# One store for tiles 16 to 31 in a matmul with scale and add, and one load of x moved ahead of addends

## The chip, the cores and the metric

The kernel runs on one core of one Trainium2 chip. The metric is the device time of one execution in microseconds (us), the median of several runs. The profile is one execution taken by the hardware profiler; its times count from the start of its span.

## What is computed

```python
batch, m, k, n = 16, 512, 1024, 768
return (scale * np.matmul(x, weight) + add_value).astype(np.float32)
```

All inputs and the output are float32, scale is 0.1. Flattened, x is 8192 rows of 1024, weight 1024 x 768, and add_value and the result 8192 rows of 768.

## The kernel before, in words

**Tiles.** The 8192 rows are cut into 64 tiles of 128. Rows are dealt out in groups of 2048: partition p of a group holds 16 consecutive rows, and tile t is row t mod 16 of every partition. Consecutive tiles of a group are therefore consecutive rows in memory, and one transfer of n tiles moves n rows in one stretch for each partition.

**Buffers.** `xs` has 16 slots for tiles of x (tile t in slot t mod 16). `ao` has 32 slots (t mod 32) that hold a tile's addends first and then, in the same place, its result, until that is stored. The addends of tile t + 32 may be loaded only when the result of tile t has been stored.

**What a tile passes through.** SyncE issues nearly all loads and stores. For every 4 tiles (a move), ScalarE and GpSimd each make 8 casts of x to bf16, into `va` (`mover`, L166, two buffers), and count them in `by_act` and `by_pool`. VectorE transposes two tiles at a time from `va` to `xt` (`turn`, L187). TensorE multiplies a tile with 8 weight loads and 16 matmuls into one of four PSUM buffers `mm` (L217, L219). VectorE then finishes two tiles in one instruction, scale * mm + addends, in place in `ao` (`finish`, L196), and counts them in `made`.

**VectorE's order.** For each group of 8 tiles it waits once for the group's addends (L201, `a_sem`), then runs finish, turn, finish, turn, and so on; the turn that follows the finish of tiles t and t + 1 prepares tiles t + 4 and t + 5. A late finish holds up the turn behind it. TensorE waits ahead of every second tile for the turn of its x and for the finish that frees its PSUM buffer (`tensor_engine`).

**SyncE's order.** `STREAM`, written out by hand, lists the transfers: "w" weights, "x" tiles of x, "a" addends, "o" results, "a+" only adjusts a count. An entry ("o", 16, 8) stores tiles 16 to 23. `sync_engine` (L99) goes through the list and issues each entry when its waits are met, so an entry that waits holds all behind it. All of these go into one DMA queue, q1. The waits (`need`, L104) are:

- x: the casts, by both engines, of the tiles whose slots it takes (for 56 to 59: of tile 43 and all before), issue at L120.
- addends: the landing of all addends issued before, and the landing of the store that frees their slots, issue at L133. For 48 to 55 this is the store that holds tile 23, for 56 to 63 the one that holds tile 31.
- results: the landing of the store two entries back, and `made` of their last tile, issue at L146.

The wait for the freeing store is found from the list itself:

```python
t = max(t for t in range(s - A_SLOTS, last + 1 - A_SLOTS) if t not in PAIR)
i = next(j for j, (a, b) in enumerate(stores) if a <= t < a + b)
need(o_sem[i % 2], 16 * (i // 2 + 1))
```

Stores from tile 48 on signal a semaphore of their own, for which the program waits at its end (L261). Tiles 14 and 15 are stored by GpSimd (L96).

Of the kernel before, what the change touches and what calls it, by code (L numbers as in the profile page):

```python
# [22 lines left out]
    ("w", 0, 4), ("w", 4, 4), ("a", 0, 8),  # L23
    ("x", 8, 8), ("a", 8, 8), ("x", 16, 8), ("a", 16, 16), ("x", 24, 8),
    ("x", 32, 8), ("a+", 16, 16), ("o", 0, 14), ("x", 40, 8), ("a", 32, 8),
    ("x", 48, 8), ("a", 40, 8), ("o", 16, 8), ("o", 24, 8), ("a", 48, 8), ("x", 56, 4),
    ("x", 60, 4), ("a", 56, 8), ("o", 32, 16), ("o", 48, 12),
    ("o", 60, 4),
]
# [267 lines left out]
```

## Time and profile before

| | |
|---|---|
| time, median of 3 runs | 206.8 us (206.76 to 206.86) |
| the profiled execution | 206.82 us, of which the span is 205.5 us |
| granted TensorE clock, mean | 0.990 |
| moved from and to HBM | 87.04 MB, 424 GB/s over the span |
| first matmul starts | 26.03 us |
| last finish (tiles 62 and 63) starts | 196.80 us |

In rows of the profile, PE is TensorE, PEld its weight loads, DVE VectorE, ACT ScalarE, POOL GpSimd; SPq is SyncE's queue of instructions, and L146 is line 146. A timeline row has the start, the duration, what ran, how often (x), and in brackets the engine's idle time just before it with what ended that. A row of DMA issues has the count, the size of one, and the median time from issue to landing. DMA and GB/s lines cut a stretch into 40 equal slices; a digit is the busy share in tenths.

### The profile page before, as it was taken

Reading aid. Unit: us, or ns where it says so; the run is one execution under the profiler, and the core shown is the slowest. Engines: PE = TensorE matmul, PEld = TensorE weight load, DVE = VectorE, ACT = ScalarE, POOL = GpSimd, SP = SyncE. Lnnn points to the kernel's source line nnn. Section 1 sums busy time; section 2 is a strip of 40 time slices with the busy share of each in tenths; the row PEclk is TensorE's granted clock in tenths of the full one; section 3 lists DMA queues with packets and bytes.
Section 4 is the critical chain, followed back from the end, with each engine's and each line's share of the span. In section 5 each row is a group of like instructions: output and inputs, shape, how many; then the busy total and the mean of one; then the engine's idle time right before and its main releaser. Section 6 shows DMA issues by size and latency. Waiting matters only on the chain.

```text
span 205.5 us, 2241 instructions
## 1 busy us (share of the span) xinstructions
PE 169.1 (82%) x1024; PEld 50.5 (25%) x512; DVE 97.8 (48%) x66; ACT 134.7 (66%) x129; POOL 137.4 (67%) x135
## 2 busy tenths in 40 slices
PE   0000099999999999999999979999999999999920
PEld 0000023332233322333223322332233332333300
DVE  0004523556555555555555346555555555555330
ACT  2049980699999906999999693959694099930000
POOL 0049994699999916999999995959694099940000
PEclk9999999999999999999999999999999999999996
DMA  7989999999999899999999999999999999998997
GB/s 287 427 375 455 421 485 408 397 439 459 440 459 459 364 453 408 408 402 410 484 390 430 446 416 470 408 435 411 454 426 408 437 459 402 517 431 364 431 459 308
DMA packets 3921, 87.04 MB, mean 424 GB/s; under 512 B 464, under 2 KB 464, under 8 KB 1104
## 3 DMA queue, kind: packets, MB, share of 16 engines
q1 hardware_dynamic: 3712, 86.25, 98.2%
q0 software_dynamic: 208, 0.79, 0.9%
q14 instruction: 1, 0.01, 0.0%
HBM read 61.87 MB, written 25.17 MB: 424 GB/s over the span
## 4 chain that ended last, share of the span: by engine, by line
PE 82%; DMA 6%; ACT 5%; DVE 2%; issue 1%; DVEq 0%; ACTq 0%
PE mm L219 82%; DMA xs<-in_x_dram 6%; ACT va L166 5%; DVE xt L187 1%; DVE ao L196 1%; DVEq L193 0%; DVEq L196 0%; DVEq L185 0%; ACTq L159 0%
## 5 line engine op out<-in xcount | busy, mean ns | idle before, releaser
L219 PE MATMUL mm<-w_bf,xt 128*128 128x512 bf16 (+1 forms) x1024 | 169.1, 329 | 27.6 <-DVE xt L187 27.6
L166 POOL CAST va<-xs 32x1024 bf16<-32x1024 f32 x128 | 135.2, 1056 | 44.3 <-DMA xs<-in_x_dram 31.1
L166 ACT CAST va<-xs 32x1024 bf16<-32x1024 f32 x128 | 133.4, 1042 | 45.3 <-DMA xs<-in_x_dram 33.0
L196 DVE SCALAR_TENSOR_TENSOR ao<-mm,ao 128x1536 f32 (+1 forms) x32 | 56.2, 1756 | 79.3 <-PE mm L219 73.4
L217 PEld LDWEIGHTS <-xt 128*128 128x128 bf16 x512 | 50.5, 99 | 145.7 <-issue 117.5
L187 DVE STREAM_TRANSPOSE xt<-va 128x1024 f32<-128x1024 f32 x32 | 39.4, 1234 | 3.3 <-ACT va L166 2.1
L180 DVE CAST w_bf<-ao 128x3072 bf16<-128x3072 f32 x2 | 4.5, 2245 | 18.1 <-DMA ao<-in_weight_dram 18.1
L155 ACT ACT_TABLE_LOAD x1 | 1.3, 1283 | 1.3 <-SPq L251 1.3
L96 POOL DMA_DIRECT2D out_dram<-ao x3 | 2.0, 671 | 0.0
L278 POOL MEMSET const-float32-0.0<- 128x1 f32 x1 | 0.1, 97 | 0.2 <-issue 0.2
L278 POOL MEMSET const-bfloat16-1.0<- 128x1 bf16 x1 | 0.1, 100 | 0.0
L278 POOL MEMSET const-float32-1.0<- 128x1 f32 x1 | 0.1, 98 | 0.0
L278 POOL MEMSET const-uint8-127<- 128x1 uint8 x1 | 0.1, 98 | 0.0
## 6 DMA issues: line engine op xcount, KB each, us to landing
xs<-in_x_dram SPq DMA_DIRECT2D x7, 4096.0 KB, 16.7
ao<-in_add_value_dram SPq DMA_DIRECT2D x6, 3072.0 KB, 17.0
ao<-in_add_value_dram SPq DMA_DIRECT2D x1, 6144.0 KB, 24.2
out_dram<-ao SPq DMA_DIRECT2D x2, 3072.0 KB, 27.5
out_dram<-ao SPq DMA_DIRECT2D x1, 6144.0 KB, 31.2
out_dram<-ao SPq DMA_DIRECT2D x1, 5376.0 KB, 28.8
out_dram<-ao SPq DMA_DIRECT2D x1, 4608.0 KB, 13.6
xs<-in_x_dram SPq DMA_DIRECT2D x2, 2048.0 KB, 21.1
```

The lines of the kernel that those rows point to most:

```text
L96: move = eng.dma_start(out_v[p:p + n, 0, pair, :], ao[p:p + n, pair, :], max_dma_last_dim=4 * N)
L155: eng.preload_act_table(mybir.ActivationFunctionType.Copy)
L166: copy(va[q % VA_BUFS][32 * b:32 * b + 32, :, a, :], src[32 * a:32 * a + 32, :, b, :]).then_inc(count, 1)
L180: eng.tensor_copy(w_bf[:, s:s + n, :], ao[:, W_AT + s:W_AT + s + n, :]).then_inc(casts, n)
L187: eng.transpose(xt[:, 2 * half:2 * half + 2, :, :].rearrange("p i c m -> p (i c m)"), va[move % VA_BUFS][:, q:q + 2 * KC, :, :].bitcast(fp ...
L196: eng.scalar_tensor_tensor(a, mm[:, q:q + 2, 0:N], float(scale), a, op0=mybir.AluOpType.mult, op1=mybir.AluOpType.add).then_inc(made, 2)
L217: eng.ldweights(x_j, tile_position=(0, 0))
L219: m = eng.add_instruction(mybir.InstMatmult(start_tensor_calc=(j == 0), stop_tensor_calc=(j == KJ - 1), tile_size=(P, P), tile_position=(0 ...
L278: nc = _bacc.Bacc("TRN2", target_bir_lowering=False, num_devices=1)
```

## The change

Two stores of 8 tiles (16 to 23 and 24 to 31) become one of 16, and the load of x of tiles 56 to 59, which stood behind the addends of 48 to 55, now stands ahead of them, right behind the merged store. The order before was: store 16 to 23, store 24 to 31, addends 48 to 55, x 56 to 59, x 60 to 63. It is now: store 16 to 31, x 56 to 59, addends 48 to 55, x 60 to 63. The addends of 48 to 55 now wait for the landing of the merged store. Nothing changes on the other engines; their instructions and order are the same.

```diff
     ("x", 32, 8), ("a+", 16, 16), ("o", 0, 14), ("x", 40, 8), ("a", 32, 8),
-    ("x", 48, 8), ("a", 40, 8), ("o", 16, 8), ("o", 24, 8), ("a", 48, 8), ("x", 56, 4),
+    ("x", 48, 8), ("a", 40, 8), ("o", 16, 16), ("x", 56, 4), ("a", 48, 8),
     ("x", 60, 4), ("a", 56, 8), ("o", 32, 16), ("o", 48, 12),
     ("o", 60, 4),
 ]
```

## Prediction

> **What bounds the kernel now.** I read the page first (engine shares, slices, queues), then the DMA issues one at a time with their time to landing, then VectorE's and TensorE's timelines around the changed stores and at the end.
>
> ```profile
> PE 169.1 (82%) x1024; PEld 50.5 (25%) x512; DVE 97.8 (48%) x66; ACT 134.7 (66%) x129; POOL 137.4 (67%) x135
> DMA  7989999999999899999999999999999999998997
> q1 hardware_dynamic: 3712, 86.25, 98.2%
> PE 82%; DMA 6%; ACT 5%; DVE 2%; issue 1%; DVEq 0%; ACTq 0%
> ```
>
> Two resources stand close to full. The chain that ended last is 82% TensorE, but SyncE's queue q1 moves 86.25 MB and fills 98.2% of what 16 DMA engines have, from the second slice to the last. So a microsecond in which q1 has nothing to move is a microsecond on the end, and TensorE matters where it holds a store back. The issues and landings show how the queue is fed. Each first fence row is an issue (start, duration), and the second fence holds, in the same order, the time from that issue to its landing.
>
> ```profile
> 102.00 0.33 SPq L133 DMA_DIRECT2D ao<-in_add_value_dram  x1
> ...
> 120.42 0.33 SPq L133 DMA_DIRECT2D ao<-in_add_value_dram  x1
> 120.80 0.43 SPq L146 DMA_DIRECT2D out_dram<-ao  x1
> 121.27 0.43 SPq L146 DMA_DIRECT2D out_dram<-ao  x1
> 144.81 0.34 SPq L133 DMA_DIRECT2D ao<-in_add_value_dram  x1
> 145.26 0.57 SPq L120 DMA_DIRECT2D xs<-in_x_dram  x1
> 145.93 0.60 SPq L120 DMA_DIRECT2D xs<-in_x_dram  x1
> 159.36 0.33 SPq L133 DMA_DIRECT2D ao<-in_add_value_dram  x1
> 159.74 0.42 SPq L146 DMA_DIRECT2D out_dram<-ao  x1
> 188.18 0.34 SPq L146 DMA_DIRECT2D out_dram<-ao  x1
> 198.63 0.33 SPq L146 DMA_DIRECT2D out_dram<-ao  x1
> ```
>
> ```profile
> ao<-in_add_value_dram SPq DMA_DIRECT2D x1, 3072.0 KB, 18.4
> ...
> ao<-in_add_value_dram SPq DMA_DIRECT2D x1, 3072.0 KB, 17.0
> out_dram<-ao SPq DMA_DIRECT2D x1, 3072.0 KB, 23.9
> out_dram<-ao SPq DMA_DIRECT2D x1, 3072.0 KB, 31.0
> ao<-in_add_value_dram SPq DMA_DIRECT2D x1, 3072.0 KB, 14.5
> xs<-in_x_dram SPq DMA_DIRECT2D x1, 2048.0 KB, 19.0
> xs<-in_x_dram SPq DMA_DIRECT2D x1, 2048.0 KB, 23.2
> ao<-in_add_value_dram SPq DMA_DIRECT2D x1, 3072.0 KB, 17.1
> out_dram<-ao SPq DMA_DIRECT2D x1, 6144.0 KB, 31.2
> out_dram<-ao SPq DMA_DIRECT2D x1, 4608.0 KB, 13.6
> out_dram<-ao SPq DMA_DIRECT2D x1, 1536.0 KB, 6.8
> ```
>
> Issue plus time gives the landings: addends of 32 to 39 at 120.4, of 40 to 47 at 137.4; stores of 16 to 23 at 144.7, of 24 to 31 at 152.3; addends of 48 to 55 at 159.3; x of 56 to 59 at 164.3, of 60 to 63 at 169.1; addends of 56 to 63 at 176.5; stores of 32 to 47 at 190.9, of 48 to 59 at 201.8, of 60 to 63 at 205.4. They land in the order of issue, spaced by their bytes: 3072 KB take 7.0 to 7.6 us, 2048 KB 4.8 to 5.0, 6144 KB 14.4. So q1 works transfer after transfer and is nowhere empty. The time of a landing is a sum of what stands ahead of it.
>
> **The change part by part.** The profiled execution took 206.82 us with a span of 205.5; the median of the runs shown is 206.8, so the sum is made on 206.82.
>
> *The merge.* Both old stores were issued back to back, at 120.80 and 121.27, so tile 31 was already finished at the first one; the merged store waits for no more than they did. One issue of 0.43 us goes from SyncE, hidden beside a full queue: 0 on the path. The bytes are the same. Whether one transfer of 6144 KB is cheaper in the queue than two of 3072: the two took 152.3 − 137.4 = 14.9 us, the single store of 32 to 47 took 190.9 − 176.5 = 14.4. Bounds are 0 and 0.5; I take 0 for the sum, since those landings carry rounding on every side, and keep 0.5 for the low end. A loss has no row here.
>
> *The wait.* The addends of 48 to 55 go into the slots of tiles 16 to 23, which were free at 144.7. Now they are free when the whole merged store has landed, at 152.3: 7.6 us later. In the old queue the store of 24 to 31 stood ahead of these addends anyway, so that alone moves no byte. It only means that something else must be in the queue while SyncE waits.
>
> *The moved load.* That is x of 56 to 59. It needs xs slots whose tiles (40 to 43) have been cast by both ScalarE and GpSimd.
>
> ```profile
> 109.25 15.27 POOL L166 CAST va<-xs 32x1024 bf16<-32x1024 f32 x14
> ```
>
> GpSimd's run of casts ends at 109.25 + 15.27 = 124.5; the next begins with tiles 44 to 47. So this load is issued at about 124.6 instead of 145.26, and stands in q1 right behind the merged store, 27 us before it is its turn. Behind SyncE's wait for these casts stands only the addends' issue, which waits until 152.3 in any case. The load covers q1 for some 4.9 us from 152.3, the addends' issue at 152.4 needs 1.0 us to start (below): no hole. x of 60 to 63 follows at 153, the addends of 56 to 63 at the landing of those of 48 to 55, as before, under cover of that x load (4.8 us).
>
> Hence the queue's order changes in one place: x of 56 to 59 and the addends of 48 to 55 swap. Old landings 159.3 (addends), 164.3 (x); new ones 157.2 (x), and 164.3 (addends), because the two together take the same 12.0 us. All later landings stay. The x load, 7 us earlier, lets ScalarE and GpSimd cast these tiles sooner, but TensorE never waited for them: after 123.72 it runs without a gap (row below). Gain 0. **The addends' loss, 5.0 us, is the question.**
>
> ```profile
> 111.86 1.76 DVE L196 SCALAR_TENSOR_TENSOR ao<-mm,ao 128x1536 f32 x1 [2.29 <-PE mm L219]
> ...
> 120.75 1.76 DVE L196 SCALAR_TENSOR_TENSOR ao<-mm,ao 128x1536 f32 x1 [5.98 <-DMA ao<-in_add_value_dram]
> 122.42 1.24 DVE L187 STREAM_TRANSPOSE xt<-va 128x1024 f32<-128x1024 f32 x1
> ...
> 160.56 1.76 DVE L196 SCALAR_TENSOR_TENSOR ao<-mm,ao 128x1536 f32 x1 [2.42 <-PE mm L219]
> ```
>
> ```profile
> 123.72 72.97 PE L219 MATMUL mm<-w_bf,xt 128*128 128x512 bf16 x448 [1.60 <-DVE xt L187]
> ```
>
> VectorE finishes tiles 48 and 49 at 160.56 today, 1.3 us after their addends landed, held by TensorE alone. With addends at 164.3 it waits for them. The trace holds the same event: the addends of 32 to 39 landed at 120.4, the finish of 32 and 33 began at 120.75 (0.35 later), the transpose behind it on VectorE (tiles 36 and 37) followed, and TensorE, which had caught up, started tile 36 at 123.72 after 1.60 us of nothing: 123.72 − 120.75 = 2.97 from finish to TensorE. Applied here: finish at 164.3 + 0.35 = 164.65, TensorE ready for tile 52 at 167.6. It would have been there at 123.72 + 16 tiles of 72.97 / 28 = 2.606 us, that is 165.4. **TensorE stalls 2.2 us**, and since it has no gap afterwards, it is late by that to the end. In other words the finish comes 4.1 us late (164.65 against 160.56), and TensorE's look-ahead hides 1.9 of it. In the old event the finish was due two tiles (5.2 us) after the one at 111.86, at 117.1; it was 3.7 late, TensorE lost 1.6, and 2.1 was hidden. The two agree within 0.2.
>
> *What late TensorE does to the queue.* The store of 48 to 59 is issued when tile 59 is finished:
>
> ```profile
> 0.73 0.38 SPq L248 DMA_DIRECT2D xs<-in_x_dram  x1
> ...
> 186.40 1.76 DVE L196 SCALAR_TENSOR_TENSOR ao<-mm,ao 128x1536 f32<-128x1536 f32 x1 [2.26 <-PE mm L219]
> ...
> 196.80 1.76 DVE L196 SCALAR_TENSOR_TENSOR ao<-mm,ao 128x1536 f32<-128x1536 f32 x1 [3.44 <-PE mm L219]
> ```
>
> 186.40 + 1.76 = 188.16, issue at 188.18; likewise 198.56 and 198.63 for the last store. Three looks at the DMA bytes in slices of 0.05 us tell how long an issue takes to move its first piece: the stretches begin at 0.7, 188.8 and 200.2, and slices of bytes count a piece at its start.
>
> ```profile
> GB/s 0 0 0 0 0 0 0 0 0 0 0 0 0 0 0 0 0 0 0 0 655 2621 0 1311 1966 655 655 0 655 0 0 655 655 0 0 0 0 0 655 0
> ...
> GB/s 0 0 0 0 0 0 0 0 0 0 0 0 0 0 0 0 0 0 0 0 737 737 737 0 737 0 1475 1475 1475 0 1475 1475 737 737 0 0 0 0 0 0
> ...
> GB/s 0 0 0 0 0 0 0 0 0 0 246 0 246 0 246 0 492 492 737 492 492 737 0 492 0 492 492 737 492 492 737 0 492 0 492 492 737 246 492 737
> ```
>
> The very first load, into an empty queue, is issued at 0.73 and starts in slice 21, between 1.70 and 1.75: **1.0 us**. The store of 48 to 59 starts in slice 21 from 188.8, between 189.80 and 189.85, when the store ahead lets go of its first engine: 1.65 after its issue, so it has 0.65 to spare. The last store starts in slice 11 from 200.2, at 200.7, 2.1 after its issue: 1.1 to spare. Both issues now come 2.2 us later. The first loses 2.2 − 0.65 = 1.5 us of empty queue; the second, counted alone, would lose 2.2 − 1.1 = 1.1, but it stands behind a store that is itself 1.5 late, so it adds nothing. Sum: 0 (merge) + 0 (x earlier) + 1.5 (empty queue at 190 us) = **206.82 + 1.5 = 208.3 us**.
>
> Bounds of the 1.5: the last store alone forces 1.1, less 0.5 if the merge saves that: 0.6. Upward, the first load took 12.1 us to land by the page's kind of row (4096 KB, from an empty queue), which by the later stores' pace of (201.8 − 190.9) / 4608 KB × 4096 = 9.7 us holds 2.4 us of starting and landing; the store of 48 to 59 would then land at 190.4 + 2.4 + 10.9 = 203.7, 1.9 late.
>
> ```profile
> xs<-in_x_dram SPq DMA_DIRECT2D x1, 4096.0 KB, 12.1
> ```
>
> The Trainium skill, "DMA: Bandwidth & Descriptors", section "Specifications", states about 0.6 us to the first byte for a transfer that SyncE issues; the trace has 1.0 here. By the page's figure the sum would be an estimated 1.1 in place of 1.5, or 207.9 us.
>
> **The rivals.**
>
> *A transfer pays a fixed price, and the merge saves one* (faster). If a saving s comes off the queue ahead of the addends, they land s earlier, the stall shrinks by s, and the end moves by 1.5 − s; this decides for faster from s = 1.9 on (0.4 us is 0.2% of 206.8). With all of the 2.4 us of the first load saved, the stall is gone, the store of 48 to 59 is issued at 188.18 into a queue that is already free and starts at 189.2 instead of 189.8: 206.2 us. Against it: 14.9 against 14.4 us above, and the last two stores, 10.9 us for 4608 KB and 3.6 for 1536, which leave 3.6 − 10.9 / 3 = 0.0 for a fixed part. The Trainium skill, same page, section "Anatomy of one DMA", gives, for transfers that GpSimd issues, a fit with about 2.0 us fixed for each; by that estimate s is 2.0 and the time 206.3. In a queue that is never empty the rows show nothing of it. Chance 0.06: 0.04 faster, 0.02 within 0.2%.
>
> *The lateness is absorbed* (no change, 206.8). The addends come 5.0 us later but VectorE is idle half of the span, and the final stores have some room. For it the look-ahead would have to hide 4.1 − 0.65 = 3.5 us of the late finish; at 120.75 it hid 2.1 of 3.7. Chance 0.07: 0.05 within 0.2%, 0.02 slightly slower.
>
> *The empty queue costs more* (208.7). The store that begins in an empty queue pays the 2.4 us of the first load: + 1.9. For it, one row; against it, that load was the first of the program. Chance 0.12.
>
> That the change doesn't take effect (x of 56 to 59 not early enough to cover the wait) would need its casts after 151; they end at 124.5. I give it nothing.
>
> **How the numbers follow.** The forecast, 208.3, has 0.75, with a range of its own from 207.4 (0.6 late) to 208.7 (1.9 late). A measurement of this kernel tells about 0.2% from no change, 206.4 to 207.2. Faster 0.04, the same 0.02 + 0.05 = 0.07, slower 0.75 + 0.12 + 0.02 = 0.89. The range of 207.3 to 208.9 holds the forecast's bounds and the dearer start, with 0.1 to 0.2 for landings known to a tenth; what it leaves out, some 0.15, is the first rival and the absorption.
>
> **What would show it.** In the profile after: x of 56 to 59 issued at 124.6 and landed at 157; the addends of 48 to 55 issued at 152.4 and landed at 164.3; a second wait of VectorE for addends, ahead of a finish at 164.65; a TensorE gap of 2.2 us that ends at 167.6; the store of 48 to 59 issued at 190.4, with q1 empty for some 1.5 us ahead of it; the last issue at 200.8; a span of 207.0. I am wrong if the addends land before 162, if TensorE shows no second gap, or if the landing of 32 to 47 moves ahead of 190.4.

## The result, and the profile after

The changed kernel takes 207.91 us (median of 14 runs, 207.78 to 209.62) against 206.83 for the kernel before, a ratio of 1.0062 over all runs (the medians alone give 1.0052) with a 95% interval of 1.0044 to 1.0081: 0.6% slower. The profiled execution took 208.01 us with a span of 206.7; its span is 1.2 us longer.

The page of the changed kernel, beside the lines shown ahead: TensorE has as much work as before, more idle time, and q1 a smaller share of the longer span. In the second line each digit is the queue's busy tenth of one fortieth; the new eights are slices 30 and 35 (150 to 155 us and 176 to 181 us). Slice 37, with 190 us in it, was an 8 before too, so this line does not show what happens there; finer slices below do.

```profile
PE 168.6 (82%) x1024; PEld 50.3 (24%) x512; DVE 97.6 (47%) x66; ACT 134.7 (65%) x129; POOL 137.4 (66%) x135
DMA  7999999999999999999999999999989999898997
q1 hardware_dynamic: 3568, 86.25, 97.5%
```

The issues of the moved load, of the addends of 48 to 55, and of the last two stores, from SyncE's timeline, and below them in the same order the DMA rows with the time to landing:

```profile
124.56 0.33 SPq L120 DMA_DIRECT2D xs<-in_x_dram  x1
...
152.26 0.33 SPq L133 DMA_DIRECT2D ao<-in_add_value_dram  x1
...
190.33 0.34 SPq L146 DMA_DIRECT2D out_dram<-ao  x1
...
200.78 0.33 SPq L146 DMA_DIRECT2D out_dram<-ao  x1
```

```profile
xs<-in_x_dram SPq DMA_DIRECT2D x1, 2048.0 KB, 32.3
...
ao<-in_add_value_dram SPq DMA_DIRECT2D x1, 3072.0 KB, 11.9
...
out_dram<-ao SPq DMA_DIRECT2D x1, 4608.0 KB, 12.4
...
out_dram<-ao SPq DMA_DIRECT2D x1, 1536.0 KB, 5.9
```

The x load lands at 156.9 instead of 164.3, the addends at 164.2 instead of 159.3, the two stores at 202.7 and 206.7 instead of 201.8 and 205.4. VectorE's waits and its finish of tiles 48 and 49, then TensorE's timeline, show what the late addends did:

```profile
DVE ao L196 <- DMA ao<-in_add_value_dram: 12.9, 2, 6.5
```

```profile
164.49 1.76 DVE L196 SCALAR_TENSOR_TENSOR ao<-mm,ao 128x1536 f32 x1 [6.48 <-DMA ao<-in_add_value_dram]
166.17 1.23 DVE L187 STREAM_TRANSPOSE xt<-va 128x1024 f32<-128x1024 f32 x1
```

```profile
123.58 41.77 PE L219 MATMUL mm<-w_bf,xt 128*128 128x512 bf16 x256 [2.08 <-DVE xt L187]
167.46 31.38 PE L219 MATMUL mm<-w_bf,xt 128*128 128x512 bf16 x192 [2.10 <-DVE xt L187]
```

VectorE now waits for addends twice (6.0 us once before). The bracket of a TensorE row holds the idle time ahead of it: one gap of 1.60 us before, two now, the second of 2.10 us at tile 52, released by the transpose of its x, which stood behind the finish, which waited for the addends. The last look is the queue at the end. The stretch from 188.8 to 192.8 in slices of 0.1 us, first of the kernel before, then of the changed one; bytes count a piece at its start:

```profile
GB/s 0 0 0 0 0 0 0 0 0 0 737 369 369 1475 737 1475 737 0 0 0 0 0 0 0 737 737 737 1475 737 1106 369 0 0 0 0 0 0 369 737 369
```

```profile
GB/s 0 0 0 0 0 0 0 0 0 0 0 0 0 0 0 0 0 0 0 0 0 0 0 2580 2949 369 0 0 0 0 0 0 0 0 0 0 0 3318 2580 0
```

Before, the 16 engines take up the store of 48 to 59 one after another between 189.8 and 190.5, each as it lets go of the store ahead, which landed at 190.9 to 191.0 in both kernels. Now none starts until 191.1, and then all within 0.3 us. That is the empty queue.

One thing was not forecast. Of the 14 runs eleven lie between 207.78 and 208.2, and three between 209.41 and 209.62. The experiments show where such a second group comes from (below). The kernel before has one too, 0.7 us higher: nine of its 14 runs lie between 206.55 and 206.97, five between 207.21 and 207.50. Between the middles of the lower groups, 206.69 and 207.89, lie 1.2 us, as between the two profiled spans. One run of the kernel before with the early addends (below) took 473.51 us, for which nothing on record gives a cause; its ratio leaves it out.

### The profile page after: what moved, and what is told of

Read it like the earlier page. It is cut to its first block, busy times and chain, and to the rows that moved or that the text cites. A ratio compares the mean times of both kernels' runs of the same rounds, so it can differ in the third digit from the quotient of the medians.

```text
span 206.7 us, 2239 instructions
## 1 busy us (share of the span) xinstructions
PE 168.6 (82%) x1024; PEld 50.3 (24%) x512; DVE 97.6 (47%) x66; ACT 134.7 (65%) x129; POOL 137.4 (66%) x135
```

## The experiments

**Order theory:** the swap makes the addends of 48 to 55 late, VectorE's finish and the transpose behind it hold TensorE, and q1 runs empty ahead of the store of 48 to 59. **Store theory:** the merged store, coarser and landing later, is the cost. **TensorE theory:** the end is late because TensorE is, whatever the queue does.

### The swap without the merge

```diff
-("o", 16, 16), ("x", 56, 4), ("a", 48, 8),
+("o", 16, 8), ("o", 24, 8), ("x", 56, 4), ("a", 48, 8),
```

> The two old stores of 8 tiles, but x of 56 to 59 ahead of the addends of 48 to 55. Order theory (the swap alone makes the addends late, TensorE stalls, q1 runs empty ahead of the store of 48 to 59): addends land near 164.2, a second TensorE gap of 2.1 us, 207.9 us. Store theory (the merge is the cost): 206.8 us.

208.83 us, ratio 1.0085 (1.0052 to 1.0117). The six runs fall in two groups: 207.80, 207.96, 208.09, which is the changed kernel's time, and 209.56, 209.61, 209.66. The profiled execution is of the upper group. Its TensorE timeline and its windows (columns: stretch and its length, then busy time of PE, PEld, DVE, ACT and POOL, the granted clock, DMA share, GB/s):

```profile
167.36 33.05 PE L219 MATMUL mm<-w_bf,xt 128*128 128x512 bf16 x192 [1.99 <-DVE xt L187]
```

```profile
164.00:168.00 4.00, 2.01 (x13) 0.57 (x6) 3.61 (x3) 2.52 (x3) 2.76 (x3) 1.00 1.05 446
168.00:172.00 4.00, 4.00 (x17) 1.02 (x8) 2.09 (x2) 1.79 (x2) 1.69 (x2) 0.57 1.06 455
```

The second stretch in the profile of the changed kernel, for comparison:

```profile
168.00:172.00 4.00, 4.00 (x26) 1.25 (x13) 2.19 (x2) 1.69 (x2) 1.59 (x2) 1.00 1.07 461
```

The gap is there with the old stores, so the swap alone makes it, and the store theory falls. After the gap the granted clock is 0.57 on average over 4 us: the trace has it at 0.5 from 168.20 to 171.61, for 3.41 us, and only 17 matmuls start in the stretch where 26 did. In all, the last 192 matmuls take 33.05 us where the changed kernel's took 31.38, 1.67 more. TensorE is then that much later still, and so is the store: the upper group is the lower one plus 1.6 us. This is the changed kernel's second group too, as far as its times show; no profile of it fell there.

### The merge without the swap

```diff
-("o", 16, 16), ("x", 56, 4), ("a", 48, 8),
+("o", 16, 16), ("a", 48, 8), ("x", 56, 4),
```

> The merged store with the old order behind it: addends of 48 to 55, then x of 56 to 59. Queue theory (the end is late by the time in which q1 is empty, wherever that is): the addends' issue waits until 152.3 with nothing left in q1, so q1 is empty for about 1.6 us near 152, the addends land near 160.7, early enough that TensorE has no second gap; the store of 48 to 59 is issued near 188.2 and finds q1 busy; about 208.1 us. TensorE theory (the end is late because TensorE ends late): no second gap, so 206.8 us. Store theory (the merged store itself costs the 1.1 us): 207.9 us.

210.63 us, ratio 1.0178 (1.0157 to 1.0199). TensorE has no second gap:

```profile
26.37 95.28 PE L219 MATMUL mm<-w_bf,xt 128*128 128x512 bf16 x576 [26.37 <-DVE xt L187]
124.01 74.66 PE L219 MATMUL mm<-w_bf,xt 128*128 128x512 bf16 x448 [2.36 <-DVE xt L187]
```

and ends at 198.67, earlier than in the changed kernel (198.84), yet the kernel is 2.7 us slower. The queue, from 149 to 159 us in slices of 0.25 us:

```profile
GB/s 1376 983 0 0 197 0 0 0 0 0 0 0 0 0 0 0 0 1081 197 98 98 0 98 393 590 393 197 688 393 492 295 492 393 393 295 688 492 98 590 393
```

From the store's last pieces (149 to 150.25) no new one starts until 153.25; then, after the first pieces of all engines (1081), hardly any starts for 1.25 us. The addends, issued at 152.35 when the store had landed, land 9.9 us later:

```profile
ao<-in_add_value_dram SPq DMA_DIRECT2D x1, 3072.0 KB, 9.9
```

In the kernel before they landed 7.0 us after that store, so 2.9 us are lost here, and the span (209.5) is 4.0 longer in all. An empty queue costs even where TensorE is not late, and the TensorE theory falls. The size was well off: 1.3 us expected, 3.9 measured (210.63 against 206.77 in that comparison). In the trace's records of the pieces, those of the addends (24 KB each) that start between 153 and 154 took 1.69 us on the mean, where such pieces took 0.91 in the kernel before. That the empty queue made them slow is not shown: with half of the cover (below) such pieces were slow in a queue that was not empty. The last 1.1 us went later: 0.85 on the addends of 56 to 63, whose pieces near 176 us took 1.36 us, and 0.3 on the store of 48 to 59. Why is not settled.

### The lateness doubled

```diff
-("x", 56, 4), ("a", 48, 8),
-("x", 60, 4), ("a", 56, 8),
+("x", 56, 4), ("x", 60, 4), ("a", 48, 8),
+("a", 56, 8),
```

> The changed kernel with x of 60 to 63 moved ahead of the addends of 48 to 55 too: the lateness doubled. Order theory: the addends land 4.9 us later than in the changed kernel, at 169.0; the second TensorE gap grows from 2.1 to 7.0 us; the store of 48 to 59 is issued near 195.2; about 212.8 us, and more where the granted clock falls after the gap. If TensorE's lateness were worth little at the end: under 210 us.

214.47 us, ratio 1.0354 (1.0325 to 1.0382); runs from 214.0 to 215.6.

```profile
172.36 34.05 PE L219 MATMUL mm<-w_bf,xt 128*128 128x512 bf16 x192 [6.90 <-DVE xt L187]
```

```profile
164.00:172.00 8.00, 1.46 (x10) 0.29 (x3) 2.60 (x2) 2.61 (x3) 2.88 (x3) 0.72 0.73 276
172.00:178.00 6.00, 5.64 (x19) 1.42 (x10) 3.09 (x3) 2.77 (x3) 2.63 (x3) 0.51 1.05 365
```

The gap is 6.90 where 7.0 was expected: the addends landed 4.9 us later than in the changed kernel, and the gap grew by 4.8. In the profiled execution, the slowest of the four (215.60), most of the rest above 212.8 is the clock, 0.51 for 6 us after the gap, 2.67 us on the last 192 matmuls (34.05 against 31.38). The other three runs were not profiled.

### The last stores cut finer

```diff
-("o", 32, 16), ("o", 48, 12),
+("o", 32, 16), ("o", 48, 8), ("o", 56, 4),
...
-                if i > 1:
+                if 1 < i < 5:
```

The second edit frees the last store from waiting for the store two entries back, which now signals another semaphore. The store of 56 to 59 still waits for the landing of 32 to 47 and is issued at 190.62.

> The changed kernel with the store of 48 to 59 cut into 48 to 55 and 56 to 59. Queue theory: the TensorE gap of 2.1 us stays and the last issue is at 200.8 as in the changed kernel, but q1 is not empty at 190; only the last store, issued at 200.8, finds q1 empty for 0.3 to 1.0 us; 207.2 us. TensorE theory: TensorE ends as late as in the changed kernel, so 207.9 us.

207.57 us, ratio 1.0054 (1.0029 to 1.0079): eight runs at 207.20 to 207.66 and four at 208.94 to 209.27, two groups again. The profiled execution (207.24 us, span 205.9) is of the lower group; TensorE's gap is still there:

```profile
167.19 31.38 PE L219 MATMUL mm<-w_bf,xt 128*128 128x512 bf16 x192 [1.98 <-DVE xt L187]
```

TensorE ends at 198.57, 1.9 us later than in the kernel before, but the span is only 0.4 longer. The pieces from 188.8 to 192.8 in slices of 0.1 us, then those from 199 to 203:

```profile
GB/s 0 0 0 0 0 0 246 0 0 737 983 737 737 492 0 246 0 0 737 983 492 737 737 0 0 246 0 492 1229 492 737 737 0 0 246 0 246 1229 737 492
```

```profile
GB/s 492 246 246 614 614 369 369 369 614 369 369 246 614 369 492 246 123 123 0 0 0 0 123 1597 246 0 0 860 983 123 0 0 1229 737 0 0 492 1229 246 0
```

With a store of 8 tiles in the queue pieces go on through 190 us, and what is left is the last store's own issue, at 200.46: no piece starts between 200.8 and 201.2, and then nearly all engines start at once. So of the changed kernel's 1.2 us the empty queue at 190 accounts for 0.8 by the two profiled spans, and for 0.5 by the middles of the lower groups (207.43 against 207.89).

### Half of the cover

```diff
-("x", 56, 4), ("a", 48, 8),
+("x", 56, 2), ("a", 48, 8), ("x", 58, 2),
...
+                if s == 58:
+                    need(half_sem, 16)
...
-                sem = x_sem[k // MOVE]
+                sem = half_sem if s == 56 else x_sem[k // MOVE]
```

The second small load also waits for the landing of the first; it was issued at 154.35, with the addends still ahead of it.

> The merged store, but only half of the moved load ahead of the addends: x of 56 and 57, then the addends of 48 to 55, then x of 58 and 59. Order theory: 1024 KB cover q1 for 2.4 us while the addends' issue needs about 0.9, so there is no empty queue; the addends land near 161.8, the finish is 1.6 us late, under the 1.9 that TensorE's look-ahead hides; no second gap, 206.6 to 206.9 us. Store theory: 207.9 us.

209.15 us, ratio 1.0108 (1.009 to 1.0126): the expectation failed. The gap shrank as it should, though to 0.84 instead of none, because the addends, issued at 152.24, landed at 162.9 and not at 161.8:

```profile
ao<-in_add_value_dram SPq DMA_DIRECT2D x1, 3072.0 KB, 10.7
```

```profile
166.21 31.38 PE L222 MATMUL mm<-w_bf,xt 128*128 128x512 bf16 x192 [0.84 <-DVE xt L190]
```

But the time went elsewhere. The addends of 56 to 63, the store of 32 to 47 and the last two stores, whose issues came at 162.91, 163.29, 189.08 and 199.53:

```profile
ao<-in_add_value_dram SPq DMA_DIRECT2D x1, 3072.0 KB, 16.1
...
out_dram<-ao SPq DMA_DIRECT2D x1, 6144.0 KB, 30.3
...
out_dram<-ao SPq DMA_DIRECT2D x1, 4608.0 KB, 15.4
...
out_dram<-ao SPq DMA_DIRECT2D x1, 1536.0 KB, 8.6
```

They land at 179.0, 193.6, 204.5 and 208.1, against 176.5, 190.9, 201.8 and 205.4 before: 2.5 to 2.7 us late from the addends on, with a queue that had work throughout. So transfers in a full queue took longer here than the same bytes did before: by the records of the pieces, the 24 KB pieces of the addends of 48 to 55 that start between 153 and 154 took 1.45 us on the mean and those of the addends of 56 to 63 near 175 us 1.3 to 1.4, instead of 0.91. Whether the small loads did that, and how, is open.

### TensorE's lead built up earlier

In both kernels the load of x of 40 to 47 was cut in two, with the addends of 32 to 39 between the halves.

```diff
-("x", 40, 8), ("a", 32, 8),
+("x", 40, 4), ("a", 32, 8), ("x", 44, 4),
```

> The kernel before with the same cut of the load of x of 40 to 47. Queue theory: TensorE ends about 1.6 us earlier, near 195, but q1 was never empty, so the end stays: 206.6 to 206.8 us. If TensorE's chain set the end, as the page's 82% reads: 205.2 us.

On the kernel before: 206.94 us, ratio 0.9999 (0.9987 to 1.0011). TensorE runs through without any gap

```profile
26.04 169.47 PE L219 MATMUL mm<-w_bf,xt 128*128 128x512 bf16 x1024 [26.04 <-DVE xt L187]
```

and ends at 195.51 instead of 196.69, which is worth nothing: the queue sets the end.

> The changed kernel, and in another place the load of x of 40 to 47 cut in two, with the addends of 32 to 39 between the halves, so that they land about 4.9 us earlier. Order theory (the loss is TensorE's lead): the first TensorE gap of 1.6 to 2.1 us near 122 goes, TensorE ends near 196.8, the store of 48 to 59 is issued near 188.7 and finds q1 busy or empty for under 0.3 us; 206.6 to 207.0 us with the swap and the merge still in. Store theory or a cost of the swap inside the queue: 207.9 us as in the changed kernel.

On the changed kernel: 209.75 us, ratio 1.0136 (1.011 to 1.0162), so this expectation was wrong, and instructively so.

```profile
26.13 138.05 PE L219 MATMUL mm<-w_bf,xt 128*128 128x512 bf16 x832 [26.13 <-DVE xt L187]
167.44 33.05 PE L219 MATMUL mm<-w_bf,xt 128*128 128x512 bf16 x192 [3.26 <-DVE xt L187]
```

TensorE comes to tile 52 at 164.18, over a microsecond sooner, and starts it at 167.44, as in the changed kernel (167.46). The landing of the addends fixes the moment; a lead only lengthens the gap, and the longer gap was followed by the lower clock (33.05 us again, 0.5 from 168.14 to 171.55). All five runs are above 209.3.

### The transpose ahead of the finish

In both kernels the first transpose of a group was put ahead of the group's wait for addends and its first finish.

```diff
     def group(i, at, last):
+            eng.wait_ge(done, i - 12)
+            turn(1, 0, i)
             eng.wait_ge(a_sem, i)
             for p in range(4):
                 finish(p, at, i + (4 * p - 12) if p < 3 else i)
-                if p < 2 or not last:
+                if p and (p < 2 or not last):
```

> The changed kernel, with VectorE's order changed at the head of each group of 8 tiles: the transpose for the group's tiles 4 and 5 ahead of the wait for its addends and of the finish of its tiles 0 and 1. Order theory (TensorE is pinned by landing of addends, then finish, then transpose on VectorE): the transpose leaves the pinned stretch, so TensorE goes on at about 164.2 + 0.3 + 1.8 = 166.3, a second gap of 0.9 us instead of 2.1; the store of 48 to 59 is issued near 189.2 and q1 is empty for 0.3 us or less; 206.8 to 207.1 us, with the loads and stores of the changed kernel untouched. If the swap or the merge costs inside the queue: 207.9 us still.

207.02 us, ratio 1.0014 (0.999 to 1.0037): eight runs at 206.59 to 207.15, level with the kernel before (206.80 in that comparison), and four at 208.27 to 208.63. The profiled execution (208.63) is of the upper four:

```profile
122.62 41.76 PE L221 MATMUL mm<-w_bf,xt 128*128 128x512 bf16 x256 [0.75 <-DVE ao L196]
166.41 33.04 PE L221 MATMUL mm<-w_bf,xt 128*128 128x512 bf16 x192 [2.02 <-DVE ao L196]
```

Tile 52 now starts at 166.41 (166.3 was expected) and the releaser is the finish itself, not the transpose. The gap is 2.02 and not 0.9, since TensorE also came 1 us earlier. The clock is at half behind it:

```profile
166.70:170.30 3.60, 3.60 (x14) 0.83 (x7) 2.37 (x2) 1.11 (x2) 0.99 (x1) 0.53 1.04 446
```

The loads and stores are those of the changed kernel, and its loss is gone in two thirds of the runs; what is left is the clock. No profile fell among those eight runs, so that their queue was not empty is read from their times.

> The kernel before with the same change of VectorE's order. Queue theory: the first TensorE gap shrinks by about 1.2 us, TensorE ends earlier, the queue is as full as it was: 206.5 to 206.8 us. If TensorE's chain set the end: 205.6 us.

On the kernel before: 206.98 us, ratio 1.0002 (0.9992 to 1.0012). The first gap is 0.35 and TensorE ends at 195.47, and that is worth nothing, as expected of a kernel with a full queue.

### Twelve and four

```diff
-("o", 16, 16), ("x", 56, 4), ("a", 48, 8),
+("o", 16, 12), ("o", 28, 4), ("a", 48, 8), ("x", 56, 4),
```

> The old order of loads, but the two stores cut as 16 to 27 and 28 to 31: a partial merge without the swap. The addends' slots come free near 148.5 with 1536 KB of stores still in q1 as cover for their issue. Queue theory: no empty queue, addends near 159.3, no second gap, 206.8 us. If a coarser store or a later issue of the addends cost by themselves: 207.3 us or more.

207.46 us, ratio 1.0027 (1.0014 to 1.0039), by the expectation's own line on the side of a cost by itself. The profiled execution, 207.94, is one of the two slowest of the twelve. TensorE has no second gap and the two last stores are issued at 188.26 and 198.71, as before; they land 14.0 and 7.9 us later, at 202.3 and 206.6. The store of 28 to 31 lands 0.4 us late, all that follows keeps that, and the last store loses another 0.7, in a queue that was full. The changed kernel shows no such loss ahead of 190 us, so this is not the cause of its empty queue.

None of these versions clearly beats the kernel before, which keeps the queue full to the end.

## Why the prediction was right

- *The merge costs and saves nothing.* Right here: the addends, second in line behind the merged store, landed at 164.2 where 164.3 was forecast; the merged store took 14.9 us in the queue (137.3 to 152.2), as the two did; and the swap with the old two stores has the same gap and the same lower group of times. That a store's cut is always free was not claimed, and the stores of twelve and four contradict it.
- *The swap exchanges two landings.* Right to 0.3 us: 156.9 and 164.2.
- *TensorE stalls 2.2 us.* 2.10 measured. The old event at 122 us was the right yardstick: finish 0.3 to 0.35 after the landing, TensorE 2.97 after the finish, in both. The forecast read the 1.9 as a look-ahead that hides lateness, which the lead experiment makes precise: it is the distance between an absolute moment and TensorE's arrival.
- *TensorE's lateness empties the queue by 1.5 us.* The mechanism was right; the size is the term that was off: 1.2 us of span, 1.1 of the median. Issue and first piece were forecast at 190.4 and 191.4 and came at 190.33 and 191.1. The 1.5 was reckoned for the first engine, which lost 1.3 to 1.4 (189.8 to 191.1 or 191.2); the engines that had let go last, at 190.5, lost 0.7 to 0.8, because all sixteen restarted together. (When they let go is taken from the kernel before.) The end follows all of them, not the first: the store of 48 to 59 lands 0.9 late. The other 0.3 of the span comes on the last store, which the forecast gave nothing, and its cause is open. The prediction's other sum, 207.9, met the median by luck: it let the store start 0.6 us after its issue, and 0.8 was measured.
- *The rivals.* A fixed price that the merge saves: no, by the landings. Lateness absorbed: no, by the gap. The empty queue costing more: not for this store, which landed at 202.7 and not at 203.7. A load took longer behind an empty queue (the merge without the swap), but there the slow pieces have no cause shown.
- *What was missing* is the clock. The forecast has no term for a TensorE pause of 2 us that is followed by some 3.4 us at half clock. The Trainium skill, "TensorE: Matmul & The Clock Gate", section "Part 1: The HAM clock gate (the "warmup" mystery)", describes a free-running window of about 3.4 us after which an idle TensorE falls to half its clock and a busy one regains it. The time at the lower clock after the gaps here, some 3.4 us, agrees with one such window. As the Trainium skill states it, with a whole idle window, a pause of 2 us would not bring it; in some of these runs it did, and the measurement decides. What decided here is read from the traces in the last section: how much of the pause fell into one window.

## What to carry to other kernels

In this queue transfers landed in order of issue, and the reordering was an exchange of two landings to 0.3 us. In such a case ask of the one that became late whether a consumer has a deadline, and of the one that became early whether anybody waited for it. When a wait is covered by another transfer, check the whole way from the late landing to the next time the queue depends on that engine; a smaller cover is not safe by itself, as the half cover cost more than the whole. Lead built up ahead of a late landing was worth nothing here, and less than nothing where it lengthened a pause. The link that paid to cut was on VectorE: a transpose that did not need the late addends stood behind a finish that did.

## What the runs showed of the hardware

- After a TensorE pause of 1.99 to 2.36 us the granted clock fell to half in some executions and not in others: three profiled executions show 1.66 to 1.69 us more on the matmuls behind it (the swap alone, the transpose ahead, the merge alone at 124 us), and the changed kernel's own profile shows none after 2.08 and 2.10. After 3.26 us the one profile shows it, and all five times agree with it. In this kernel's three upper runs, if the cause is the same, it turns a loss of 1.1 us into one of 2.7.
- Where the pause lies decides. In all twelve traces the moments at which the granted clock changed lie on a grid of 3.41 us, whose place differs from execution to execution: the stretches at half clock behind a gap are 3.41 us long, 10.24 (three times that) with the lateness doubled, and the stretches at full clock between two changes are whole multiples. Take the windows of this grid that began at full clock, from the first change of clock (near 30 us) to the end. Of the 28 that held 0.2 to 1.92 us of TensorE idle time none was followed by a fall; all 16 that held 1.99 us or more were. The changed kernel's pause of 2.10 was cut by the grid into 0.7 and 1.4, while in the swap alone all of the 1.99 lay in one window. No run moved the grid on purpose, so this is a reading after the fact, and it would explain the two groups of times.
- It would explain the upper group of the kernel before as well, whose pause at 122 us was 1.60 in its profile and up to 2.36 in versions that differ from it up to there only in the stores issued at 121 us. None was profiled, but the two versions of that kernel in which the pause is gone or 0.35 us long have no such group (11 runs up to 207.08 and 12 up to 207.25).
- A store into an empty queue started 0.8 to 0.9 us after its issue on all engines at once and then ran at its usual pace. A load into an empty queue at 152 us also started after 0.9 us, but its first pieces took 1.69 us instead of 0.91, its second pieces were late, and it took 9.9 us from issue to landing for 3072 KB.
- Transfers in a full queue were not always equally fast: with the loads of 2 tiles the addends of 56 to 63 landed 2.5 us late, and with the stores of twelve and four the end lost 1.1 us. In the first case 24 KB pieces took 1.3 to 1.4 us near 175 us instead of 0.91. Nothing here settles whether the size of the pieces or the way in which the engines are staggered does it.
